# Query and key split into float16 parts once, in the feature-major stage, and copied per head in the attention; GpSimd makes two of eight high parts of the probabilities

## The chip, the core and the metric

The kernel runs on one core of one Trainium2 chip. The core has five engines that work beside each other, each through its own list of instructions in a fixed order: TensorE (PE, matrix products, results go to PSUM), VectorE (DVE), ScalarE (ACT, functions and copies), GpSimd (POOL, elementwise work in SBUF) and SyncE (SP, which issues the transfers here). Where an instruction needs the result of another engine, it waits for a semaphore, and what stands behind it in its list waits too. The metric is the device time of one execution in microseconds.

## What is computed

One encoder layer for 1024 tokens of width 1024 in float32: a modulated RMS norm, one input projection, two groups of heads, an output projection, and a gated residual.

```python
xn = rmsnorm(h, norm_g) * (1 + scale) + shift          # scale, shift, gate from c
proj = xn @ w_in
u_pool, g_pool, q_lat, kv_lat, k_rope_raw, g_attn = split(proj)
y_pool = multiscale_pool(u_pool) * silu(g_pool)        # 4 groups of 128 channels, windows 2, 4, 8, 16
q = rmsnorm(q_lat) @ w_uq ; kv = rmsnorm(kv_lat) @ w_ukv     # 8 heads, q and k of 96 = 64 + 32 rotary
q, k = rmsnorm(q), rmsnorm(k) ; rotary on the last 32
o = softmax(q @ k.T * 96**-0.5) @ v                    # dense, all 1024 positions
y = concat(y_pool, o * silu(g_attn)) @ w_out
out = h + gate * y
```

The precision of float32 is kept by splitting operands in a high and a low part and summing three products: high by high, high by low, low by high. In the attention the parts are float16, elsewhere they are a 32-bit format of TensorE.

## The kernel before, in words

Tokens are tiled by 128 (t from 0 to 7) where features lie along a row ("token-major"), and features by 128 where tokens lie along a row ("feature-major"). The program has these stages, one behind the other on TensorE:

1. **Latents.** The normed input is split into `xh` and `xl`, and the 416 latent columns of the projection are made token-major.
2. **Up-projection** (`up_tok`, one call a token tile). From the latents come q (`QT`, 8 token tiles by 8 heads by 96, float32), the 64 plain features of k (`KT`, the same shape) and v. The sums of squares for the per-head norms are gathered, and `up_norm` makes the factors `rqk`.
3. **Feature-major stage.** The other 12 column tiles of the projection. Tiles 2g and 2g+1 are gate and input of pooling group g, tiles 8 to 11 the gates of the attention. `fm_mm` issues 48 matmuls of 128x512 for a tile (L170): 8 slices of the contraction, for each the products (`whi`,`xh`), (`whi`,`xl`), (`wlo`,`xh`), for two halves of the tokens. The weights come in by a transfer, ScalarE rounds the high part (`whi`, L147), VectorE subtracts for the low one (`wlo`, L148). Both have two buffers, so the weights of tile i can be split once TensorE has done tile i-2. GpSimd multiplies the raw weights by `shift` and folds them (L152, L154), and a small matmul turns the result into the tile's bias (`psb`, L160). `rb_mul` (L527) takes a tile out of PSUM. For the pooling input of group g that is the tile `u`; GpSimd adds its shifted copies, one add more in each group (`s`, L609 and L614), VectorE finishes the means (L617, L618, L621), ScalarE and VectorE split the result (`dh` L624, `dl` L625), and `pool_map` multiplies it on TensorE (`pps`, L640) and into the gate (L641). Between these stand the calls of `up_tail(t)`, eight in all: VectorE multiplies q and k of token tile t by their norm factors and turns the rotary part, in place in `QT` and `KT` (seven instructions, L644 to L654).
4. **Attention.** Eight heads of eight jobs each; a job is 128 queries by all keys (jobs 0 to 3 of a head) or 256 keys by 512 queries (jobs 4 to 7). For each head the parts of q and k must first be made, token-major in a pair of tiles (`src00`, `src01` for even heads, `src1h`, `src1l` for odd ones), and turned by transposing transfers (`turn`). `conv_hi` rounds a head's columns of `KT` or `QT` to float16 (L705 on ScalarE, L707 on VectorE), `conv_lo` subtracts to get the low part (L711). For heads 0 and 1 this is done on the way into the attention, for head h+2 in steps 4 to 7 of head h: VectorE rounds k at step 4 and q at step 6, GpSimd subtracts one half of a tile at each of the four steps. Column 0 of a tile holds one extra row, a bound for the scores, which `prep_max` finds (L730, L733) at four steps of the head before.
   For job i: `scores` (six matmuls, L800 or L804, in two buffers of PSUM; in jobs 0 to 3 a maximum by VectorE, L808 and L809), one step later `expo` (ScalarE, L819: the probabilities p, float32), two steps later `p_hi` (ScalarE rounds p to float16, `ph`, L824) and `p_lo` (the rest, L831, on GpSimd; on VectorE for jobs 1 and 7, whose p lies in PSUM), and six steps later `attend` (L849, L850). `out_copy` (L868, L869) and `out_norm` (L875, L879) finish four jobs. In the last head the parts of the output projection's operands are made beside it (`out_split` L935, L937; `y_split` L914, L916, L918).
5. **Output projection**, eight tiles of 128 features, and the residual.

From the up-projection to the start of the attention the order of each engine's list is set by a scheduler when the program is built: it goes by its own estimates of what is ready when. In the latents and from the attention on (`manual_schedule`) the list is as the loops write it. Pools of buffers set the rest: the feature-major tiles and the `pps` take turns in seven banks of PSUM, `u`, `ra` and `rbt` have one buffer each, and p in SBUF has three.

## Time and profile before

| | us |
|---|---|
| median of 3 runs | 500.09 (499.56 to 500.47) |
| the profiled execution, its own time | 500.05 |
| its span, first to last instruction | 498.3 |
| busy: PE, DVE, ACT, POOL | 464.9, 355.9, 253.8, 234.4 |
| feature-major stage | about 115 to 222 |
| attention | about 225 to 410 |
| output projection | to the end |

All times in the profile count from the start of the span, which leaves 1.75 us of the execution's own time outside. Matmuls are pipelined, so a row's duration on TensorE overlaps that of the next; the distance from start to start is what one costs. The same holds, for less than a tenth of a microsecond, on VectorE. What stands in square brackets behind a row is how long the engine sat idle before it, and what ended that.

### The profile page before, as it was taken

To read this page: it belongs to the slowest core of one execution; us is meant where nothing else is said; L and a number is where in the kernel's file an instruction comes from. 1 tells how busy PE (TensorE), PEld (TensorE's weight loads), DVE (VectorE), ACT (ScalarE), POOL (GpSimd) and SP (SyncE) were. 2 spreads that over 40 slices of the span, in tenths; PEclk is the share of its full clock that TensorE was granted. 3 is DMA by queue.
4 is the path that set the end of the run, shared out by engine and by line. 5 is a ranking of instruction groups with operands and counts; after the bars stand their busy time and mean duration, and the time that the engine had idled before them with its cause. 6 is when DMAs were issued, how large, how long until landed. Compare 5 with 4: busy or idle time off the path is not lost.

```text
span 498.3 us, 7657 instructions
## 1 busy us (share of the span) xinstructions
PE 464.9 (93%) x2956; PEld 355.0 (71%) x2956; DVE 355.9 (71%) x565; ACT 253.8 (51%) x338; POOL 234.4 (47%) x190
## 2 busy tenths in 40 slices
PE   5999998999999999999989888898898969999997
PEld 3999876898888888785555555555555658888886
DVE  4888849999999853577677887877867985913221
ACT  3756038993203030226878888888899861001000
POOL 1950040201242949448869796787869780000000
PEclk9999999999999999999999999999999999999999
DMA  8894442000102110144786779779982836753333
GB/s 300 332 307 159 171 142 65 6 1 7 47 1 91 34 58 27 57 86 95 170 148 138 162 145 176 152 151 163 224 175 63 160 113 231 276 182 129 126 128 126
DMA packets 117046, 66.33 MB, mean 133 GB/s; under 512 B 105873, under 2 KB 107793, under 8 KB 117010
## 3 DMA queue, kind: packets, MB, share of 16 engines
q1 hardware_dynamic: 117010, 65.85, 49.9%
q8 instruction: 23, 0.38, 0.3%
q14 instruction: 13, 0.11, 0.1%
HBM read 35.43 MB, written 4.19 MB: 80 GB/s over the span
## 4 chain that ended last, share of the span: by engine, by line
PE 49%; DVE 22%; ACT 10%; POOL 10%; issue 5%; DMA 3%; SPq 0%; ACTq 0%; DVEq 0%; POOLq 0%
PE ops L974 14%; PE fps L170 8%; PE st L800 4%; PE pq L548 3%; ACT ph L824 3%; PE lps L234 3%; DVE bp L808 3%; POOL fraw L152 3%; ACT p L819 3%; DMA wlr<-in_w_lat 2%; PE rs L730 2%; PE av L849 2%; PE st L804 2%; POOL s L614 2%; DVE ph L831 2%
## 5 line engine op out<-in xcount | busy, mean ns | idle before, releaser
L831 POOL TENSOR_TENSOR ph<-p,ph 128x1024 f16<-128x1024 f32 x49 | 105.9, 2168 | 13.1 <-ACT ph L824 10.2
L170 PE MATMUL fps<-xh,whi 128*128 128x512 f32 x192 | 62.0, 404 | 0.5 <-ACT whi L147 0.5
L170 PE MATMUL fps<-xh,wlo 128*128 128x512 f32 x192 | 59.3, 390 | 0.1
L170 PE MATMUL fps<-xl,whi 128*128 128x512 f32 x192 | 59.3, 390 | 0.0
L800 PE MATMUL st<-q,k 97*128 97x512 f16 x192 | 49.5, 379 | 6.7 <-ACT p L819 6.6
L804 PE MATMUL st<-k,q 97*128 97x512 f16 x192 | 48.2, 379 | 8.0 <-ACT p L819 6.4
L824 ACT ACTIVATE ph<-p 128x1024 f16<-128x1024 f32 x49 | 51.7, 1055 | 0.5
L152 POOL TENSOR_TENSOR fraw<-fraw,shift 128x1024 f32<-128x1024 f32 x7 | 22.7, 3237 | 60.8 <-DVE wlo L148 53.8
L808 DVE TENSOR_REDUCE bp<-st 128x1 f32<-128x1024 f32 x32 | 39.0, 1220 | 5.2 <-PE st L804 3.4
L170 PEld LDWEIGHTS fps<-xh,whi 128*128 128x128 f32 x192 | 35.5, 189 | 9.0 <-ACT whi L147 1.0
L170 PEld LDWEIGHTS fps<-xh,wlo 128*128 128x128 f32 x192 | 36.0, 188 | 8.1 <-DVE wlo L148 0.5
L170 PEld LDWEIGHTS fps<-xl,whi 128*128 128x128 f32 x192 | 36.1, 188 | 7.7
L935 ACT ACTIVATE owhi<-oraw 128x1024 fp32r<-128x1024 f32 (+1 forms) x10 | 8.8, 885 | 54.0 <-DMA oraw<-in_w_out 54.0
L819 ACT ACTIVATE p<-st,bp,esc 128x1024 f32<-128x1024 f32 x25 | 30.1, 1204 | 9.4 <-DVE bp L809 9.0
L804 PEld LDWEIGHTS <-q 97*128 97x128 f16 x192 | 16.6, 97 | 25.6 <-issue 10.9
L800 PEld LDWEIGHTS <-k 97*128 97x128 f16 x192 | 16.6, 97 | 21.5 <-issue 8.3
L624 ACT ACTIVATE dh<-s 128x1024 fp32r<-128x1024 f32 x4 | 4.2, 1062 | 51.9 <-DVE s L621 51.9
L819 ACT ACTIVATE p<-st,ebias,esc 128x1024 f32<-128x1024 f32 x24 | 28.9, 1203 | 2.5 <-PE st L800 1.3
L850 PE MATMUL av<-VT,ph 128*128 128x65 f16 x256 | 26.4, 193 | 2.9 <-POOL ph L831 2.9
L849 PE MATMUL av<-VT,pt 128*128 128x129 f16 x256 | 28.0, 221 | 0.8 <-DMA pt<-ph 0.8
L849 PE MATMUL av<-VT,ph 128*128 128x129 f16 x256 | 27.7, 221 | 0.2 <-DVE rb L869 0.2
L850 PEld LDWEIGHTS <-ph 128*128 128x128 f16 x256 | 22.6, 98 | 7.1 <-POOL ph L831 3.1
(297 smaller groups left out, 1142.5 us busy)
## 6 DMA issues: line engine op xcount, KB each, us to landing
fraw<-in_w_fm SPq DMA_DIRECT2D x12, 512.0 KB, 3.7
asc<-in_ada_sc SPq DMA_DIRECT2D x8, 512.0 KB, 6.0
xr<-in_xT SPq DMA_DIRECT2D x8, 512.0 KB, 5.3
ash<-in_ada_sh SPq DMA_DIRECT2D x8, 512.0 KB, 6.8
oraw<-in_w_out SPq DMA_DIRECT2D x8, 512.0 KB, 5.1
xres<-in_xT SPq DMA_DIRECT2D x8, 512.0 KB, 5.0
agt<-in_ada_gt SPq DMA_DIRECT2D x8, 512.0 KB, 5.7
out_dram<-xres SPq DMA_DIRECT2D x7, 512.0 KB, 3.0
```

The costliest lines, as they stand in the source:

```text
L152: G.tensor_tensor(pb, pb, shift.unsqueeze(2).broadcast_to([P, NK, P]), ALU.mult)
L170: T.matmul(ps[n], w[:, k, :], x_[k][:, n * 512:(n + 1) * 512], start=(k == order[0] and j == 0), stop=(k == order[-1] and j == 2))
L234: T.matmul(ps[:, :LAT], l[k][:, ts_], r[k], start=(k == 0 and i == 0), stop=(k == NK - 1 and i == 2))
L800: T.matmul(stt[i][:, n], l[:HW, kt * P:(kt + 1) * P], r[:HW, 0:512], start=(a == 0), stop=(a == 2))
L804: T.matmul(stt[i][:, n], l[:HW, qt * P:(qt + 1) * P], r[:HW, n * 512:(n + 1) * 512], start=(a == 0), stop=(a == 2))
L808: V.tensor_reduce(bps[i], stt[i], AX.XY, ALU.max)
L819: A.activation(pfs[i], st, AF.Exp, bias=bps.pop(i) if hf else ebias, scale=esc)
L824: A.activation(pas[i][:, 0], pfs[i], AF.Copy)
L831: (V if in_psum(i) else G).tensor_tensor(pas[i][:, 1], pfs[i], pas[i][:, 0], ALU.subtract)
L849: T.matmul(o_, hi, VT[:, kt, h, 0:129], start=kt == 0 and qt % 2 == 0, stop=False, skip_group_check=True)
L850: T.matmul(o_[:, 0:65], lo, VT[:, kt, h, 0:65], start=False, stop=kt == NK - 1, skip_group_check=True)
L974: T.matmul(ps[d][n], w_[:, k, :], y_[k][:, n * 512:(n + 1) * 512], start=(k == 0 and j == 0), stop=(k == NK - 1 and j == 2))
```

## The change

`up_tail` no longer works in place. For q and then for k of a token tile it builds the normed and turned values in a new float32 tile (`fq` or `fk`, one buffer that both share). ScalarE then rounds that tile to float16 and VectorE subtracts, and the two float16 parts are written over the float32 row of `QT` or `KT`, which is twice as wide: first the high parts of all heads, then the low ones. In the attention, `conv_hi` and `conv_lo` are replaced by `gather`, a copy of both parts of a head, float16 to float16, 1536 elements a partition: on VectorE for head 0 and, at steps 4 and 6, for head h+2, on ScalarE for head 1. GpSimd's four half-tile subtractions in each of six heads are gone. `p_hi` of jobs 3 and 5 of a head (`HG`), from the second head on, moves from ScalarE to GpSimd.

```diff
+HG = (3, 5)
...
+    def halves(w, t):
+        return (QT, KT)[w][:, t].rearrange("p h d -> p (h d)").bitcast(F16).rearrange(
+            "p (a h d) -> p a h d", a=2, h=H)
+
     def up_tail(t):
-        V.tensor_tensor(QT[:, t], QT[:, t], rqk[:, 0, t, :].unsqueeze(2).broadcast_to([P, H, HD]), ALU.mult)
-        V.tensor_tensor(KT[:, t, :, 0:64], KT[:, t, :, 0:64],
-                        rqk[:, 1, t, :].unsqueeze(2).broadcast_to([P, H, 64]), ALU.mult)
-        V.tensor_tensor(KT[:, t, :, 64:], krr[:, t, :].unsqueeze(1).broadcast_to([P, H, 32]),
-                        rqk[:, 1, t, :].unsqueeze(2).broadcast_to([P, H, 32]), ALU.mult)
...
+        for w in range(2):
+            f_ = dp.tile([P, H, HD], F32, tag="fq", name=f"f{'qk'[w]}{t}")
+            if w == 0:
+                V.tensor_tensor(f_, QT[:, t], rqk[:, 0, t, :].unsqueeze(2).broadcast_to([P, H, HD]), ALU.mult)
...
+                V.tensor_tensor(ra, f_[:, :, 64:], TA[:, t, :].unsqueeze(1).broadcast_to([P, H, 32]), ALU.mult)
+                V.tensor_tensor(rbt, f_[:, :, 64:], TB[:, t, :].unsqueeze(1).broadcast_to([P, H, 32]), ALU.mult)
+                V.tensor_tensor(f_[:, :, 64:80], ra[:, :, 0:16], rbt[:, :, 16:32], ALU.subtract)
+                V.tensor_tensor(f_[:, :, 80:96], ra[:, :, 16:32], rbt[:, :, 0:16], ALU.add)
+            else:
...
+            p_ = halves(w, t)
+            A.activation(p_[:, 0], f_, AF.Copy)
+            V.tensor_tensor(p_[:, 1], f_, p_[:, 0], ALU.subtract)
...
-    def conv_hi(h, w, eng, t0=0, t1=NK):
-        o_, i_ = srcs[h % 2][w][:, 0, t0:t1, 1:HW], (QT, KT)[w][:, t0:t1, h, :]
+    def gather(h, w, eng):
+        i_ = (QT, KT)[w].rearrange("p t h d -> p (t h d)").bitcast(F16).rearrange(
+            "p (t a h d) -> p a t h d", t=NK, a=2, h=H)[:, :, :, h, :]
+        o_ = srcs[h % 2][w][:, :, :, 1:HW]
...
-    def conv_lo(h, w, eng, t0=0, t1=NK):
...
     for w in (1, 0):
-        conv_hi(0, w, V)
-        conv_lo(0, w, V)
+        gather(0, w, V)
         turn(0, w)
...
-        conv_hi(1, w, A)
-        conv_lo(1, w, G)
+        gather(1, w, A)
...
     def p_hi(i):
...
-        A.activation(pas[i][:, 0], pfs[i], AF.Copy)
+        if i % 8 in HG and i > 7:
+            G.tensor_copy(pas[i][:, 0], pfs[i])
+        else:
+            A.activation(pas[i][:, 0], pfs[i], AF.Copy)
...
             if step % 2 == 0:
-                conv_hi(h + 2, 3 - step // 2, V)
-            conv_lo(h + 2, 3 - step // 2, G, step % 2 * 4, step % 2 * 4 + 4)
+                gather(h + 2, 3 - step // 2, V)
```

The scheduler puts the longer tails elsewhere. Line numbers of the changed kernel are used in the rows of the change. TensorE's list is the same in both kernels. On VectorE, late in the feature-major stage, these rows stand before the change between the weights of tile 8 and the means of pooling group 3 (`u3` is that group's input, `wlo9` the low weights of tile 9):

```order
L148 TENSOR_TENSOR wlo8_1669<-fraw8_1666,whi8_1668 128x1024
L527 TENSOR_TENSOR u3_1738<-fps7_0_1672,rb_79 128x512
L527 TENSOR_TENSOR u3_1738<-fps7_1_1673,rb_79 128x512
L641 SCALAR_TENSOR_TENSOR yp2_1226<-pps20_1728,small_64,yp2_1226 128x512
L641 SCALAR_TENSOR_TENSOR yp2_1226<-pps21_1733,small_64,yp2_1226 128x512
L148 TENSOR_TENSOR wlo9_1788<-fraw9_1785,whi9_1787 128x1024
```

And these in the change, up to `u3`:

```order
L149 TENSOR_TENSOR wlo8_1699<-fraw8_1696,whi8_1698 128x1024
L653 TENSOR_TENSOR fq5_1788<-QT_797,rqk_114 128x768
L656 TENSOR_TENSOR ra5_1790<-fq5_1788,TA_111 128x256
L657 TENSOR_TENSOR rbt5_1791<-fq5_1788,TB_112 128x256
L658 TENSOR_TENSOR fq5_1788<-ra5_1790,rbt5_1791 128x8x16
L659 TENSOR_TENSOR fq5_1788<-ra5_1790,rbt5_1791 128x8x16
L667 TENSOR_TENSOR QT_797<-fq5_1788,QT_797 128x768
L661 TENSOR_TENSOR fk5_1798<-KT_798,rqk_114 128x8x64
L663 TENSOR_TENSOR fk5_1798<-krr_113,rqk_114 128x8x32
L667 TENSOR_TENSOR KT_798<-fk5_1798,KT_798 128x768
L653 TENSOR_TENSOR fq6_1803<-QT_797,rqk_114 128x768
L528 TENSOR_TENSOR u3_1768<-fps7_0_1702,rb_79 128x512
```

Before, all eight tails stood ahead of `u3`, all but the last rows of tail 7 ahead of `u2`; now tail 5 and the first row of tail 6 stand between `wlo8` and `u3`, and tails 6 and 7 behind it. Right behind an L663 or L659 the row L667 waits for ScalarE's copy of the tile just written.

On ScalarE the rounding of tile 10's weights stood behind one function of a gate:

```order
L624 ACTIVATE dh3_1754<-s3_3_1749 128x1024
L676 ACTIVATE gT0_1848<-gT0_1848,bias_fm_80 128x1024
L147 ACTIVATE whi10_1854<-fraw10_1852 128x1024
```

In the change two of the new copies stand among these:

```order
L625 ACTIVATE dh3_1784<-s3_3_1779 128x1024
L666 ACTIVATE KT_798<-fk6_1813 128x768
L689 ACTIVATE gT0_1896<-gT0_1896,bias_fm_80 128x1024
L666 ACTIVATE QT_797<-fq7_1818 128x768
L148 ACTIVATE whi10_1902<-fraw10_1900 128x1024
```

`whi10` has moved behind the copy of `fq7`, whose rows on VectorE stand behind those of tail 6 and around the two rows that take tile 8 (`gT0`) out of PSUM.

On GpSimd in the attention, steps 4 to 7 of the second head (`ph112` is the low part of job 2 of head 1, `ph113` of job 3, `ph100` to `ph102` of jobs 4 to 6), before:

```order
L711 TENSOR_TENSOR src1l_2046<-KT_798,src1l_2046 128x4x96
L831 TENSOR_TENSOR ph112_2439<-p112_2407,ph112_2439 128x1024
L711 TENSOR_TENSOR src1l_2046<-KT_798,src1l_2046 128x4x96
L831 TENSOR_TENSOR ph113_2494<-p113_2442,ph113_2494 128x1024
L711 TENSOR_TENSOR src1h_2045<-QT_797,src1h_2045 128x4x96
L831 TENSOR_TENSOR ph100_2514<-p100_2492,ph100_2514 128x1024
L711 TENSOR_TENSOR src1h_2045<-QT_797,src1h_2045 128x4x96
```

and in the change:

```order
L843 TENSOR_TENSOR ph112_2478<-p112_2447,ph112_2478 128x1024
L834 CAST ph113_2532<-p113_2481 128x1024
L843 TENSOR_TENSOR ph113_2532<-p113_2481,ph113_2532 128x1024
L843 TENSOR_TENSOR ph100_2551<-p100_2530,ph100_2551 128x1024
L891 TENSOR_TENSOR op0_2442<-rb_79,rec00_2582 128x4x64
L834 CAST ph101_2587<-p101_2549 128x1024
L843 TENSOR_TENSOR ph101_2587<-p101_2549,ph101_2587 128x1024
```

The low part of job 2 no longer stands behind a subtraction that waits for VectorE's rounding of k, and two new casts stand ahead of the low parts of jobs 3 and 5.

More of the change, by code (lines that the diff above doesn't have):

```diff
@@ L647, in up_tail @@
-        V.tensor_tensor(KT[:, t, :, 64:], krr[:, t, :].unsqueeze(1).broadcast_to([P, H, 32]),
-                        rqk[:, 1, t, :].unsqueeze(2).broadcast_to([P, H, 32]), ALU.mult)
-        ra = dp.tile([P, H, 32], F32, tag="ra", name=f"ra{t}")
-        rbt = dp.tile([P, H, 32], F32, tag="rbt", name=f"rbt{t}")
-        V.tensor_tensor(ra, QT[:, t, :, 64:], TA[:, t, :].unsqueeze(1).broadcast_to([P, H, 32]), ALU.mult)
-        V.tensor_tensor(rbt, QT[:, t, :, 64:], TB[:, t, :].unsqueeze(1).broadcast_to([P, H, 32]), ALU.mult)
@@ L653, in up_tail @@
-        V.tensor_tensor(QT[:, t, :, 64:80], ra[:, :, 0:16], rbt[:, :, 16:32], ALU.subtract)
-        V.tensor_tensor(QT[:, t, :, 80:96], ra[:, :, 16:32], rbt[:, :, 0:16], ALU.add)
+        for w in range(2):
+            f_ = dp.tile([P, H, HD], F32, tag="fq", name=f"f{'qk'[w]}{t}")
+            if w == 0:
+                V.tensor_tensor(f_, QT[:, t], rqk[:, 0, t, :].unsqueeze(2).broadcast_to([P, H, HD]), ALU.mult)
+                ra = dp.tile([P, H, 32], F32, tag="ra", name=f"ra{t}")
+                rbt = dp.tile([P, H, 32], F32, tag="rbt", name=f"rbt{t}")
+                V.tensor_tensor(ra, f_[:, :, 64:], TA[:, t, :].unsqueeze(1).broadcast_to([P, H, 32]), ALU.mult)
[3 more added lines that the diff above has]
+            else:
+                V.tensor_tensor(f_[:, :, 0:64], KT[:, t, :, 0:64],
+                                rqk[:, 1, t, :].unsqueeze(2).broadcast_to([P, H, 64]), ALU.mult)
+                V.tensor_tensor(f_[:, :, 64:], krr[:, t, :].unsqueeze(1).broadcast_to([P, H, 32]),
+                                rqk[:, 1, t, :].unsqueeze(2).broadcast_to([P, H, 32]), ALU.mult)
+            p_ = halves(w, t)
+            A.activation(p_[:, 0], f_, AF.Copy)
+            V.tensor_tensor(p_[:, 1], f_, p_[:, 0], ALU.subtract)
@@ L707, in conv_hi @@
             eng.tensor_copy(o_, i_)
-    def conv_lo(h, w, eng, t0=0, t1=NK):
-        s_ = srcs[h % 2][w]
-        eng.tensor_tensor(s_[:, 1, t0:t1, 1:HW], (QT, KT)[w][:, t0:t1, h, :], s_[:, 0, t0:t1, 1:HW], ALU.subtract)
     def turn(h, w):
```

## The prediction

> **What bounds the kernel now.** I read the busy times by stretch first, then the chain of waits in order of time, then each engine's rows where the chain runs. The feature-major stage from the first row of the first tail (125.56 us) to the low weights of tile 10 (211.43); columns: stretch, length, busy PE, PEld, DVE, ACT, POOL, clock, DMA:
>
> ```profile
> 125.56:211.43 85.87, 85.32 (x378) 69.74 (x377) 65.35 (x111) 15.97 (x15) 47.57 (x31) 1.00 0.14 45
> ```
>
> TensorE looks like the bound. The chain that ended last (start, length, what) says otherwise:
>
> ```profile
> 159.40 10.00 POOL fraw L152
> ...
> 209.13 1.05 ACT whi L147
> 210.20 1.24 DVE wlo L148
> ```
>
> It runs through GpSimd's folds and sums and VectorE to `whi10` and `wlo10`, and tile 10 waits for them. The rows of the engines around it:
>
> ```profile
> 210.22 0.73 PE L170 MATMUL fps<-xh,whi 128*128 128x512 f32 x2 [0.54 <-ACT whi L147]
> 179.05 0.16 DVE L617 TENSOR_TENSOR s<-s,small 128x4 f32<-128x4 f32 x1 [6.21 <-POOL s L614]
> 201.17 1.24 DVE L617 TENSOR_TENSOR s<-s,small 128x8 f32<-128x8 f32 x1 [10.00 <-POOL s L614]
> 134.16 2.39 DVE L645 TENSOR_TENSOR KT<-KT,rqk 128x512 f32<-128x512 f32 x1
> 133.50 2.49 POOL L152 TENSOR_TENSOR fraw<-fraw,shift 128x1024 f32<-128x1024 f32 x1 [3.44 <-DVE wlo L148]
> 185.54 1.90 POOL L152 TENSOR_TENSOR fraw<-fraw,shift 128x1024 f32<-128x1024 f32 x1 [4.71 <-DVE wlo L148]
> 213.54 2.85 POOL L154 TENSOR_TENSOR fraw<-fraw 128x512 f32<-128x512 f32 x3
> ```
>
> TensorE reaches tile 10 only 0.54 us ahead of its weights: a VectorE that comes later has no cover there. VectorE is idle for 85.87 - 65.35 = 20.5 us of the stretch, but most of it is two waits for GpSimd's sums (6.21 and 10.00). And the two engines hold each other up: L152 takes 1.90 us alone and 10.00 beside VectorE's tails (159.40); L645 takes 2.39 beside an L152, and 0.68 in the next fence. A whole fold alone is 1.90 + 2.85 = 4.75.
>
> **The tails.** An undisturbed token tile; the distance from start to start is what a row costs:
>
> ```profile
> 139.38 0.94 DVE L644 TENSOR_TENSOR QT<-QT,rqk 128x768 f32<-128x768 f32 x1
> 140.25 0.28 DVE L653 TENSOR_TENSOR QT<-ra,rbt 128x128 f32<-128x128 f32 x1
> ...
> 140.66 0.68 DVE L645 TENSOR_TENSOR KT<-KT,rqk 128x512 f32<-128x512 f32 x1
> 141.26 0.41 DVE L647 TENSOR_TENSOR KT<-krr,rqk 128x256 f32<-128x256 f32 x1
> 141.59 0.41 DVE L651 TENSOR_TENSOR ra<-QT,TA 128x256 f32<-128x256 f32 x1
> ...
> 142.26 1.28 DVE L527 TENSOR_TENSOR u<-fps,rb 128x512 f32<-128x512 f32 x2
> ```
>
> A tail is 142.26 - 139.38 = 2.88 us of VectorE. The forms that the change adds (a subtraction to float16, a copy to float16) stand in the making of heads 0 and 1; with them come the handover from VectorE to ScalarE and back, and the other rows that the sum needs:
>
> ```profile
> 217.60 0.95 DVE L711 TENSOR_TENSOR src<-QT,src 128x768 f16<-128x768 f32 x1
> 218.47 1.21 DVE L148 TENSOR_TENSOR wlo<-fraw,whi 128x1024 fp32r<-128x1024 f32 x1
> 224.81 0.83 ACT L705 ACTIVATE src1h<-QT 128x768 f16<-128x768 f32 x1
> 128.58 1.22 DVE L621 SCALAR_TENSOR_TENSOR s<-s,u 128x1024 f32<-128x1024 f32 x1
> 129.91 1.06 ACT L624 ACTIVATE dh<-s 128x1024 fp32r<-128x1024 f32 x1 [2.83 <-DVE s L621]
> 131.01 1.23 DVE L625 TENSOR_TENSOR dl<-s,dh 128x1024 fp32r<-128x1024 f32 x1
> 148.87 0.21 DVE L633 CAST pwh<-pwr 128x128 fp32r<-128x128 f32 x1
> 185.38 1.28 DVE L527 TENSOR_TENSOR u<-fps,rb 128x512 f32<-128x512 f32 x2
> 186.57 1.41 DVE L641 SCALAR_TENSOR_TENSOR yp<-pps,small,yp 128x512 f32<-128x512 f32 x2
> 208.07 1.15 ACT L676 ACTIVATE gT<-gT,bias_fm 128x1024 f32<-128x1024 f32 x1 [2.62 <-DVE gT L527]
> ```
>
> A subtraction costs 218.47 - 217.60 = 0.87 us, two a tail: 2.88 + 1.74 = 4.62. ScalarE has room (15.97 us busy of 85.87), but its copy stands between VectorE's last row on `fq` or `fk` and the subtraction: 0.11 us to ScalarE (L621 ends at 129.80, L624 starts at 129.91), 0.83 for the copy, 0.04 back (130.97 to 131.01). The row ahead is busy 0.41 where its follower could start after 0.33, so a wait that nothing fills is 0.08 + 0.98 = 1.06 us. `fq` and `fk` share one buffer and VectorE's list is fixed, so only what the scheduler put between can fill it. Nothing stands between for k of tiles 0, 4 and 5 and for q of tiles 3 and 5: five bare waits ahead of `u3`.
>
> I add up VectorE's time in three sections.
>
> *First tail to the end of `u3`*: 125.56 to 186.66 before, 61.1 us. Eight tails stood in it (8 x 2.88 = 23.0); now six and one row (6 x 4.62 + 0.87 = 28.6): +5.6. Five bare waits: +5.3. The wait for group 2's sums (6.21) shrinks, because VectorE comes to it later: behind `u2` GpSimd needs three sums of 1.95 (next fence), 5.85, and up to 2.0 more while VectorE's subtraction and `wlo7` run; VectorE fills 3.4 of it (L641 1.4, subtraction 0.87, `wlo7` 1.14). That leaves 2.5 to 4.5; I take 4.4, because L152's 10.00 shows GpSimd giving way: -1.8. The blocking elsewhere I keep as it was. Together +9.1: `u3` ends near 195.8.
>
> *`u3` to group 3's sums*: 186.66 to 201.17 before, 14.5 us, with the fold of tile 8 and a part of tile 9's in the way.
>
> ```profile
> 190.98 1.97 POOL L609 TENSOR_TENSOR s<-u 128x1038 f32<-128x1038 f32 x1
> 193.02 3.90 POOL L614 TENSOR_TENSOR s<-s 128x1036 f32<-128x1036 f32 x2
> ```
>
> Now the fold of tile 8 is over by then and that of tile 9 stands behind the sums. Four sums are 1.97 + 3 x 1.95 = 7.8 us, and up to 2.5 more beside `ra` and `rbt` (0.67), `wlo9` (1.14), two rotary rows (0.41) and the pool weights (some 0.35). I take 9.8, towards the upper end as above: -4.7.
>
> *The sums to the end of `wlo10`*: 201.17 to 211.43 before, 10.3 us. VectorE now does edges and mean (1.28), subtracts q of tile 6 (0.87), does `fk6` and `dl3` (0.60 + 1.14 + 0.33), waits (1.06), subtracts (0.87), starts `fq7` (0.87), takes tile 8 out of PSUM (1.2) with `ra` and `rbt` between (0.67): 8.9. Then ScalarE's gate (0.11 + 1.06), the copy of `fq7` (0.8), `whi10` (1.05), and `wlo10` (1.24): 13.2. Of blocking by a fold the old section held 1.1 (L617 1.24 at 201.17, 0.16 at 179.05), and tile 9's fold still runs beside it, so I keep 1.1: 14.3, +4.0.
>
> Sum: 9.1 - 4.7 + 4.0 = **+8.4 us**, all of it TensorE's, which waits at tile 10. Lower bound: GpSimd's rows all slip into the new waits (group 2's wait falls by 4.4 more, the second section to 7.8, no blocking in the third): 8.4 - 4.4 - 2.0 - 1.1 = +0.9. Upper bound: the fold of tile 8 slips behind `u3` and that of tile 9 blocks fully: 8.4 + 4.75 + 3.65 = +16.8. I stay in the middle; it is nearest to the blocking that the trace has.
>
> Between tile 10 and the attention, the last tail, its waits and two copies in place of two casts and two subtractions cost VectorE some 1.5 us more. The cover is the 2.7 us for which the turned q of head 0 lay ready (221.95 to 224.67):
>
> ```profile
> 219.72 2.23 SPq L722 DMA_TRANSPOSE q<-src  x1
> ...
> 224.67 0.61 PE L730 MATMUL rs<-k,q 97*128 97x512 f16 x2
> ```
>
> If that cover were gone it would be +1.5; I take 0. ScalarE's two wider copies for head 1 replace GpSimd's subtractions behind the same casts: 0.
>
> **The attention.** ScalarE loses two casts a head, GpSimd trades four half subtractions (0.86 each) for two casts. The question is whether TensorE waits for these. Rows from two neighbouring heads, and one from the last:
>
> ```profile
> 281.52 0.56 DVE L707 CAST src<-KT 128x768 f16<-128x768 f32 x1
> 265.48 2.25 DVE L707 CAST src1h<-QT 128x768 f16<-128x768 f32 x1
> 265.17 2.14 POOL L831 TENSOR_TENSOR ph<-p,ph 128x1024 f16<-128x1024 f32 x1
> 280.02 1.06 ACT L824 ACTIVATE ph<-p 128x1024 f16<-128x1024 f32 x1
> 282.15 0.86 POOL L711 TENSOR_TENSOR src<-KT,src 128x384 f16<-128x384 f32 x1 [3.15 <-DVE src L707]
> 268.91 0.59 PE L730 MATMUL rs<-k,q 97*128 97x512 f16 x2 [0.53 <-DVE src L733]
> 275.02 1.46 PE L804 MATMUL st<-k,q 97*128 97x512 f16 x6 [1.19 <-ACT p L819]
> 280.04 0.81 PE L800 MATMUL st<-q,k 97*128 97x512 f16 x3 [0.88 <-ACT p L819]
> 407.67 0.20 PE L850 MATMUL av<-VT,ph 128*128 128x65 f16 x1 [2.95 <-POOL ph L831]
> ```
>
> TensorE's two long waits of a head (1.19, 0.88) are for the exponentials of jobs 0 and 2, which stand behind the high parts of jobs 7 and 1 on ScalarE. The casts that leave it are those of jobs 3 and 5: gain 0.
>
> The copy of k is where VectorE may lose. Before, GpSimd was idle there (3.15), waiting for the rounding, which took 0.56. Now the low part of job 2 can start when ScalarE's row of 280.02 ends (281.08), ahead of VectorE at 281.52, and runs 2.1 us. VectorE would stand until 283.2, 1.7 us, as its rounding of q stood behind the L831 of 265.17 (2.25 in place of 0.56). The maxima behind it (L733) come late by that, but TensorE already waits 0.53 for them later in the head, and the wait of q's copy gets shorter as that of k's grows, since the low part of job 3 is then further on. I take +0.3 a head for six heads, +1.8; bounds -0.5 a head (the 0.53 gone) and +1.7 a head.
>
> The copy has twice the elements of the cast; from L633 (128 elements, 0.21) to L707 (768, 0.56) an element costs 0.55 ns, so 1536 take 0.56 + 0.42 = 0.98, between 0.56 if that is bytes and not elements, and 0.95 + 768 x 1.02 ns = 1.73 if it runs like the two-input rows (0.95 for 768, 1.21 for 1024). I take 0.98, by the row that is also a copy in SBUF; the 0.4 more is in the +0.3. GpSimd's cast of 1024 lies between 0.86 (a row of 384) and 2.14; half of the two-input row, 1.1, is nearest for one input. Two of them fit in the four subtractions' 3.4. In the last head, where no subtractions were, GpSimd ends TensorE's wait of 2.95; the casts take 2.2 us more there, but in place of waits for ScalarE: -1 to +2, I take 0.
>
> Attention: **+1.8**, bounds -3 and +10 to +12.
>
> [...]
>
> **Sum.** The profiled execution took 500.05 us, the median is 500.09, so nothing is to be corrected: 500.05 + 8.4 + 1.8 = 510.3, say **510**.
>
> **Rivals.**
> - *The slack takes it.* The new work is 16 x 0.87 = 13.9 us and VectorE idles 20.5. For it speaks the idle time, against it that this is waiting for sums which start behind `u3`, and `u3` moves back. Then the lower bounds hold: 500.05 + 0.9 - 3 = 498.
> - *Half of it.* GpSimd's folds slip into the new waits, the sums start as they did after `u3`: +4, attention 0: 504.
> - *The copy of k decides in every head.* 500.05 + 8.4 + 6 x 1.7 = 518.7. It decides once the low part of job 2 starts ahead of the copy by more than VectorE's gaps in these steps (0.53 and the like) can take.
>
> **Chances.** Forecast (506 to 515) 0.58, half 0.17, copy of k 0.12, slack 0.13. The range that leaves out 2 in 10 is 502 to 516. About 1 us, 0.2%, is what a measurement of this kernel can tell from no change: of the slack's 0.13 I give 0.09 to faster and 0.04 to the same; all the rest, 0.87, is slower.
>
> **What would show it.** Right: `u3` (L528) ends near 196 and `wlo10` (L149) near 220, TensorE stands some 8 us more ahead of tiles 9 and 10, VectorE waits about 1 us for L666 in five to eight places, and the attention's length stays within 2 us, with L722 for k at over 2 us. Wrong: `wlo10` ends before 214; or TensorE's waits for the exponentials of jobs 0 and 2 shrink though only casts of jobs 3 and 5 left ScalarE; or L722 for k grows and the heads grow with it.

## The result, and the profile after

The changed kernel takes 516.45 us (median of 6 runs, 515.73 to 518.25), the kernel before, measured beside it, 500.28 (499.56 to 503.08, 6 runs): a ratio of 1.032, 95% interval 1.029 to 1.035. The forecast was 510, with a range of 502 to 516. The sign is right, the size is about 6 us short, and the time lies just above the range. The profiled execution of the change has a span of 514.0 us, 15.7 more than before.

The three sections of the feature-major stage that the prediction summed, in the changed kernel (stretch, length, busy PE, PEld, DVE, ACT, POOL, clock, DMA): first tail to the end of `u3`, to the first row on group 3's sums, to the end of `wlo10`:

```profile
124.81:199.59 74.78, 72.77 (x321) 59.36 (x321) 65.89 (x97) 22.26 (x24) 29.41 (x23) 1.00 0.13 40
199.59:212.41 12.82, 6.01 (x20) 4.50 (x19) 12.79 (x11) 0.84 (x1) 12.35 (x6) 0.73 0.07 27
212.41:226.76 14.35, 9.27 (x40) 6.74 (x38) 11.73 (x20) 4.73 (x5) 2.27 (x2) 1.00 0.10 37
sum 101.95, PE 88.06 PEld 70.60 DVE 90.41 ACT 27.84 POOL 44.03; mean PE 29.35 PEld 23.53 DVE 30.14 ACT 9.28 POOL 14.68
```

TensorE was busy for 85.32 of 85.87 us of this stage before; now it is for 88.06 of 101.95. It stands still for 13.9 us, at these places (rows of TensorE with what it waited for, the last one at the start of the attention):

```profile
174.62 0.74 PE L171 MATMUL fps<-xh,wlo 128*128 128x512 f32 x2 [0.93 <-DVE wlo L149]
...
199.05 0.50 PE L171 MATMUL fps<-xh,whi 128*128 128x512 f32 x1 [0.96 <-DVE u L528]
206.82 1.22 PE L171 MATMUL fps<-xh,wlo 128*128 128x512 f32 x2 [6.80 <-DVE wlo L149]
220.86 0.35 PE L161 MATMUL psb<-ones,fraw 128*128 128x1 f32 x2 [2.27 <-DVE bias_fm L162]
225.55 0.74 PE L171 MATMUL fps<-xh,whi 128*128 128x512 f32 x2 [2.82 <-ACT whi L148]
242.50 0.61 PE L741 MATMUL rs<-k,q 97*128 97x512 f16 x2 [0.85 <-DMA q<-src]
```

What VectorE did around these waits, rows in order of time:

```profile
193.51 0.96 DVE L667 TENSOR_TENSOR QT<-fq,QT 128x768 f16<-128x768 f32 x1 [0.91 <-ACT QT L666]
...
196.44 0.96 DVE L667 TENSOR_TENSOR KT<-fk,KT 128x768 f16<-128x768 f32 x1 [0.91 <-ACT KT L666]
197.44 0.96 DVE L653 TENSOR_TENSOR fq<-QT,rqk 128x768 f32<-128x768 f32 x1
198.31 1.28 DVE L528 TENSOR_TENSOR u<-fps,rb 128x512 f32<-128x512 f32 x2
...
201.79 2.13 DVE L657 TENSOR_TENSOR rbt<-fq,TB 128x256 f32<-128x256 f32 x1
203.84 2.92 DVE L149 TENSOR_TENSOR wlo<-fraw,whi 128x1024 fp32r<-128x1024 f32 x1
206.69 2.46 DVE L658 TENSOR_TENSOR fq<-ra,rbt 128x128 f32<-128x128 f32 x1
209.07 1.98 DVE L659 TENSOR_TENSOR fq<-ra,rbt 128x128 f32<-128x128 f32 x1
...
212.41 0.15 DVE L618 TENSOR_TENSOR s<-s,small 128x8 f32<-128x8 f32 x1
```

`u3` (L528 at 198.31) comes 12.9 us later than before (185.38). Behind it stands no wait for GpSimd's sums any more, where 10.00 us stood. Instead four rows, one behind the other, take 1.98 to 2.92 us each, about as long as one of GpSimd's sums (1.92, 1.97, 1.96 and 3.24): L658 takes 2.46 us, against 0.28 in a quiet place, and `wlo9` 2.92 against 1.22. GpSimd ran its four sums in the same time:

```profile
199.68 1.92 POOL L610 TENSOR_TENSOR s<-u 128x1038 f32<-128x1038 f32 x1 [6.76 <-DVE u L528]
201.67 7.33 POOL L615 TENSOR_TENSOR s<-s 128x1036 f32<-128x1036 f32 x3
```

From here on a row's **hold-up** is its duration less the shortest that a row of its form has in any run of this study, added up over rows; differences of less than 0.05 us, which rows show without GpSimd's work too, are left out, and a sum holds to some 0.2 us. A row's own price, under "rows", is that shortest duration less 0.09 us, for the overlap with the next; "gaps" is what remains. VectorE's time in the first section, worked out in this way (us):

| kernel | length | rows | held up | waits for sums | waits for ScalarE | gaps |
|---|---|---|---|---|---|---|
| before | 61.1 | 45.3 | 7.3 | 6.2 | 0.8 | 1.5 |
| change | 74.8 | 50.8 | 12.1 | 3.6 | 4.9 | 3.4 |

In the second section VectorE is held up for 8.9 us (1.6 before). Over the whole way to the copy of q for head 0 it is 23.5 us against 11.1.

### The profile page after: what moved, and what is told of

It is laid out like the page before. It is cut to its first block, busy times and chain, and to the rows that moved or that the text cites. A ratio compares the mean times of both kernels' runs of the same rounds, so it can differ in the third digit from the quotient of the medians.

```text
span 514.0 us, 7647 instructions
## 1 busy us (share of the span) xinstructions
PE 469.2 (91%) x2956; PEld 356.4 (69%) x2956; DVE 384.2 (75%) x579; ACT 255.1 (50%) x340; POOL 227.1 (44%) x178
## 4 chain that ended last, share of the span: by engine, by line
PE 53%; DVE 24%; ACT 9%; POOL 6%; DMA 4%; issue 3%; SPq 0%; ACTq 0%; DVEq 0%; POOLq 0%
PE ops L986 14%; PE fps L171 8%; PE st L809 6%; PE st L813 5%; PE av L861 3%; PE pq L549 3%; ACT p L828 3%; PE rs L741 2%; POOL ph L843 2%; DMA wlr<-in_w_lat 2%; PE lps L235 2%; DVE fq L653 2%; PE pk L559 2%; ACT ph L836 2%; DVE wlo L149 2%
## 5 line engine op out<-in xcount | busy, mean ns | idle before, releaser
L843 POOL TENSOR_TENSOR ph<-p,ph 128x1024 f16<-128x1024 f32 x49 | 107.2, 2194 | 39.4 <-ACT ph L836 35.2
L171 PE MATMUL fps<-xh,wlo 128*128 128x512 f32 x192 | 61.2, 401 | 7.9 <-DVE wlo L149 7.7
L171 PE MATMUL fps<-xh,whi 128*128 128x512 f32 x192 | 63.4, 411 | 3.8 <-ACT whi L148 2.8
L153 POOL TENSOR_TENSOR fraw<-fraw,shift 128x1024 f32<-128x1024 f32 x7 | 16.3, 2330 | 71.9 <-DVE wlo L149 59.8
L836 ACT ACTIVATE ph<-p 128x1024 f16<-128x1024 f32 x35 | 36.9, 1054 | 0.5
L809 PEld LDWEIGHTS <-k 97*128 97x128 f16 x192 | 16.5, 97 | 21.2 <-issue 7.3
L744 DVE TENSOR_REDUCE src<-rs 128x1 f16<-128x1024 f32 x16 | 19.6, 1224 | 10.1 <-PE rs L741 9.3
```

The source lines that it names most:

```text
L153: G.tensor_tensor(pb, pb, shift.unsqueeze(2).broadcast_to([P, NK, P]), ALU.mult)
L171: T.matmul(ps[n], w[:, k, :], x_[k][:, n * 512:(n + 1) * 512], start=(k == order[0] and j == 0), stop=(k == order[-1] and j == 2))
L744: V.tensor_reduce(s_[:, 0, qt, 0:1], ps, AX.XY, ALU.max, negate=True)
L809: T.matmul(stt[i][:, n], l[:HW, kt * P:(kt + 1) * P], r[:HW, 0:512], start=(a == 0), stop=(a == 2))
L836: A.activation(pas[i][:, 0], pfs[i], AF.Copy)
L843: (V if in_psum(i) else G).tensor_tensor(pas[i][:, 1], pfs[i], pas[i][:, 0], ALU.subtract)
```

## The experiments

Times are medians, ratios go against the kernel before, each with its 95% interval. Diffs are against the changed kernel where nothing else is said. The first theory was that VectorE is now the bound, by its subtractions, its waits for ScalarE and more blocking by GpSimd than I had allowed for.

**Two buffers for `fq` and `fk`.**

```diff
-            f_ = dp.tile([P, H, HD], F32, tag="fq", name=f"f{'qk'[w]}{t}")
+            f_ = dp.tile([P, H, HD], F32, tag=f"f{w}", name=f"f{'qk'[w]}{t}")
```

> The changed kernel with a buffer of its own for fq and one for fk, so that q of a tile need not wait for k's subtraction and the other way round. Theory (VectorE is the bound of the feature-major stage, by its subtractions, its bare waits for ScalarE and the blocking by GpSimd): most of the waits of 0.91 us for L666 fill with other rows, eight to ten of them, so wlo10 ends 4 to 8 us earlier than 226.8 and the time is 508 to 513. Rival A (the waits for ScalarE are nearly all of the loss): 500 to 506. Rival B (the order of VectorE's list decides, u3 stands one tail further back in it here): 516 or more.

513.35 us, 1.026 (1.021 to 1.031). VectorE's waits for ScalarE in the first section fall from 4.9 to 1.7 us, but `u3` ends no earlier (its section is 76.3 us): held up 9.7, waits for sums 6.8. Waits for ScalarE are not nearly all of the loss, so rival A falls. The theory's 508 to 513 was just missed, and `wlo10` ends at 224.2, only 2.6 us earlier where it had 4 to 8.

**The high part on VectorE.**

```diff
-            A.activation(p_[:, 0], f_, AF.Copy)
+            V.tensor_copy(p_[:, 0], f_)
```

> The changed kernel with the high part of q and k copied by VectorE instead of ScalarE: no handover, but 16 copies of 0.56 us (9 us) more on VectorE. Theory (VectorE bound): 16 copies of 0.5 us come on and eight to ten waits of 0.91 go, so about the same, 514 to 518. Rival A (the waits for ScalarE are nearly all): 505 to 510. Rival C (what GpSimd takes from VectorE is the larger part, and a copy waits for GpSimd as other rows do): over 518.

520.14 us, 1.040 (1.037 to 1.043). There is no wait for ScalarE left in the first section (4.9 us in the changed kernel), but with the copies (0.55 us each where nothing holds them up) it is 79.4 us long, 17.7 of them hold-ups. The theory's "about the same" was missed; rival C's number came in.

**No low part, first attempt.**

```diff
-            V.tensor_tensor(p_[:, 1], f_, p_[:, 0], ALU.subtract)
+            A.activation(p_[:, 1], f_, AF.Copy, scale=0.0)
```

> The changed kernel without the subtractions of the low part in the feature-major stage: ScalarE writes zeros there (so the low parts of q and k are left out of the result). VectorE loses 16 x 0.87 = 13.9 us and its waits for the high part. Theory (VectorE bound): the whole delay of the stage goes, 498 to 502. Rival C (GpSimd's blocking of the small rotary rows is the larger part, and these rows stay): half of it goes, 506 to 510.

ScalarE writes zeros in place of the low parts. 510.44 us, 1.020 (1.016 to 1.025). This is near rival C's 506 to 510, but the run doesn't tell: with one buffer, VectorE now waits for two copies of ScalarE in place of one:

```profile
165.26 0.69 DVE L661 TENSOR_TENSOR fk<-KT,rqk 128x512 f32<-128x512 f32 x1 [1.65 <-ACT QT L667]
167.93 0.96 DVE L653 TENSOR_TENSOR fq<-QT,rqk 128x768 f32<-128x768 f32 x1 [1.65 <-ACT KT L667]
```

In the first section 12 us of such waits took the place of the subtractions. So it was run again with two buffers:

> The changed kernel without the subtractions of the low part (ScalarE writes zeros, the low parts of q and k are left out of the result) and with a buffer each for fq and fk, so that the second copy on ScalarE does not hold VectorE up as it did with one buffer (waits of 1.65 us). Theory (subtractions, waits for ScalarE and what is queued behind them make the delay): 498 to 503. Rival C (blocking of the rotary rows by GpSimd is the larger part, whatever VectorE has to do besides): 506 or more.

499.60 us, 0.998 (0.995 to 1.002). Against the 513.35 with two buffers and the subtractions (two runs, 512.31 and 514.39) these cost 13.75 us, 16 x 0.86: every one at about its full price, although VectorE had idle time. In the profiled executions the first scores come 12.75 us earlier (227.04 against 239.79).

**The order of VectorE's list.** Two edits: the weights ahead, and the tails of tiles 5 to 7 queued behind `u3` (`u_last[3]` is the last row that takes `u3` out of PSUM).

```diff
-            fm_w[i + 1] = fm_weights(i + 1)
+            with tc.high_priority():
+                fm_w[i + 1] = fm_weights(i + 1)
```

> The changed kernel with the weight rows (copy to whi, subtraction to wlo) given precedence in the scheduler, so that wlo9 stands on VectorE ahead of the rotary rows of tile 6 that wait for GpSimd's sums. Theory (VectorE's whole list up to wlo10 bounds): TensorE's wait of 6.80 us for wlo9 goes, and the wait at tile 10 grows by as much; the time stays within 2 us, 514 to 518. Rival B (the order of the list decides): 6.8 us less, 509 to 511.

```diff
-        if gi:
+        if gi == 3:
+            with tc.issue_after(u_last[gi]):
+                up_tail(2 * gi - 1)
+                up_tail(2 * gi)
+        elif gi:
             up_tail(2 * gi - 1)
             up_tail(2 * gi)
-    up_tail(7)
+    with tc.issue_after(u_last[3]):
+        up_tail(7)
```

> The changed kernel with the tails of token tiles 5, 6 and 7 queued on VectorE behind u3, as far as u3 allows; nothing else is changed. In the changed kernel TensorE had finished tile 7 near 185 us, but u3 came only at 198.3, since the fixed list has it behind tail 5. Theory (VectorE's whole work up to the copies of head 0 bounds): u3 ends near 189, wlo10 by 214, TensorE's waits at tiles 9 and 10 nearly go, but the tails are then unfinished: the copies of head 0 end near 232 and the first scores come at 236 to 240 instead of 242.5, so 510 to 514. Rival B (the order of the list decides): the first scores near 230, 501 to 505. Rival D (the order is without effect): 516.

519.57 us, 1.039 (1.032 to 1.045), and 519.18 us, 1.036 (1.033 to 1.039). In the first, TensorE's wait for `wlo9` shrinks from 6.80 to 0.77 us and `wlo10` ends at 225.6 instead of 226.8, but TensorE then waits 9.29 us for VectorE at the small matmul of a bias (220.44); nothing is won, and the time is above the 514 to 518 that I expected. In the second `u3` comes at 187.85. The delay only moves, to VectorE's wait for the sums and to TensorE's first scores:

```profile
202.70 1.84 DVE L621 TENSOR_TENSOR s<-s,small 128x8 f32<-128x8 f32 x1 [6.27 <-POOL s L618]
...
244.06 1.04 PE L749 MATMUL rs<-k,q 97*128 97x512 f16 x2 [9.76 <-DMA q<-src]
```

Neither order helps, which fits the theory that VectorE's whole list up to the copies of head 0 decides. My own 510 to 514 for the second was too low, since the fold of tile 8 came to stand ahead of the sums on GpSimd.

**Without GpSimd's work.** The sums, and the folds from tile 4 on, left out in both kernels:

```diff
-            fm_fold(pb)
+            if i < 4:
+                fm_fold(pb)
...
-        s_ = gp.tile([P, S + 16], F32, tag="gT0", name=f"s{gi}_0")
-        G.tensor_tensor(s_[:, 1:S + 15], u[:, 0:S + 14], u[:, 1:S + 15], ALU.add)
-        lo_, m = 1, 1
-        for lev in range(gi):
+        s_ = u
+        for lev in ():
```

> The changed kernel without GpSimd's running sums (the unsummed tile takes their place) and without its folds from tile 4 on, so the pooled branch and the biases are left out of the result. Against the kernel before with the same left out. Theory (some 7 us of the delay is VectorE's small rows waiting for GpSimd, the rest subtractions and waits for ScalarE): this kernel loses both the waits for the sums and the blocking and comes to 500 to 506, 2 to 8 us above its counterpart. Rival A (subtractions and waits for ScalarE alone): 508 or more, over 10 us above its counterpart.

> The kernel before with the same left out (GpSimd's running sums, and its folds from tile 4 on). TensorE was busy for 85.3 of 85.9 us of the feature-major stage, so nothing is to be had there: 497 to 500 by every theory.

497.96 us, 0.994 (0.992 to 0.996), and 499.20 us, 0.996 (0.995 to 0.998). This is the central pair: without these rows of GpSimd the change costs nothing in the stage, with all 16 subtractions, all rounding on ScalarE and the single buffer as they are. (It is even some 1.2 us faster, and that comes behind the first scores: 271.65 us from there to the end against 274.08.) Nor is it the order of the list: as in the changed kernel, tails 0 to 5 and the first row of tail 6 stand ahead of `u3`. VectorE still has waits of 0.91 us, but they lie beside TensorE's tiles; it takes `u3` out of PSUM at 185.17:

```profile
183.31 0.96 DVE L666 TENSOR_TENSOR KT<-fk,KT 128x768 f16<-128x768 f32 x1 [0.91 <-ACT KT L665]
...
185.17 0.68 DVE L529 TENSOR_TENSOR u<-fps,rb 128x512 f32<-128x512 f32 x1
```

TensorE's waits on the way to the attention come to 0.5 us, as in the kernel before the change, and the first scores come at 224.51 (224.67 before the change). So "subtractions and waits for ScalarE" is no cause by itself, and my own theory, which left 2 to 8 us between the two kernels, fell short as well. Half of GpSimd's work was left out next, by one of the two edits each:

> The changed kernel without GpSimd's folds from tile 4 on (the biases are left out of the result); the running sums stay. Theory now (VectorE's rows with two inputs from SBUF wait for GpSimd's instructions, 23.5 us in the changed kernel against 11.1 before, from the first tail to the copy of q of head 0; subtractions and waits for ScalarE alone fit into VectorE's idle time): folds and sums are each about half of GpSimd's work, so the excess falls to about half, 10 to 14 us, and the time to 500 to 506. Rival E (the sums alone do it, since they stand in the chain): 510 or more.

> The changed kernel without GpSimd's running sums (the unsummed tile takes their place, so the pooled branch is left out of the result); the folds stay. Theory: excess of VectorE 8 to 12 us, no waits for the sums, 498 to 503. Rival E (the sums alone do it): 498, with hardly any excess left beside the folds.

502.27 us, 1.003 (1.001 to 1.005), and 501.54 us, 1.001 (0.999 to 1.003). Leaving out either half is enough to come within 2 us of the kernel before, so it isn't the sums alone (rival E). Hold-ups to the copy of q are 9.5 and 14.6 us, where I had expected 10 to 14 and 8 to 12.

**GpSimd's work in shorter pieces.** The same work, each sum and the multiplication of each fold in four parts, the first addition of a fold in two:

```diff
-        G.tensor_tensor(pb, pb, shift.unsqueeze(2).broadcast_to([P, NK, P]), ALU.mult)
+        for a in range(0, NK, NK // 4):
+            b = a + NK // 4
+            G.tensor_tensor(pb[:, a:b], pb[:, a:b], shift[:, a:b].unsqueeze(2).broadcast_to([P, b - a, P]), ALU.mult)
...
+        def g_add(o, a, b, l, h):
+            cs = [l + (h - l) * i // 4 for i in range(4 + 1)]
+            for x, y in zip(cs, cs[1:]):
+                G.tensor_tensor(o[:, x:y], s_in[:, x - a:y - a], s_in[:, x + b:y + b], ALU.add)
...
-            G.tensor_tensor(n_[:, l2:h2], s_[:, l2 - m:h2 - m], s_[:, l2 + m:h2 + m], ALU.add)
+            s_in = s_
+            g_add(n_, m, m, l2, h2)
```

> The changed kernel with every running sum and every fold of GpSimd cut into pieces (sums and the multiplication of a fold into four, its first addition into two), the same work in shorter instructions; nothing is left out. Theory F (a row of VectorE waits until the running GpSimd instruction is over, one instruction each in turn): a blocked row loses some 0.5 us instead of up to 2, VectorE's excess falls from 23.5 to 6 to 12 us and the time to 501 to 508. Rival G (the two share one rate, and only the sum of their work counts): excess 20 or more, 514 to 518.

> The same cut of GpSimd's work and a buffer each for fq and fk. Theory F with the waits for ScalarE filled: 498 to 504, at or below the kernel before. Rival G: 511 to 515, as with two buffers alone.

513.86 us, 1.027 (1.025 to 1.029), and with two buffers 516.25 us, 1.031 (1.029 to 1.033). In the first, the single hold-up shrinks as theory F had it: beside the fold of tile 8 a rotary row takes 0.8 us where it took 2.00 (L656 at 188.22 in the change):

```profile
190.50 0.83 DVE L668 TENSOR_TENSOR rbt<-fq,TB 128x256 f32<-128x256 f32 x1
...
191.87 0.82 DVE L670 TENSOR_TENSOR fq<-ra,rbt 128x128 f32<-128x128 f32 x1
```

Hold-ups up to the copy of q fall from 23.5 to 13.5 us, just above F's 12, but the time by only 2.6, since the sums come later: VectorE's waits for them in the first section rise from 3.6 to 7.7 us. Hold-ups plus waits for sums are 15.2 us there with the cut and 15.7 without. Rival G came nearest on the time (514 to 518) though not on the hold-ups (20 or more); F was right about the row. With two buffers both missed: the time is above G's 511 to 515, and hold-ups plus waits for sums are 18.6 us in the first section, 10.8 of them waits.

**16 rows more in the kernel before**, which has no rounding on ScalarE in its tails: with two inputs from SBUF, or with one, at the same places of the list.

```diff
         V.tensor_tensor(QT[:, t, :, 80:96], ra[:, :, 16:32], rbt[:, :, 0:16], ALU.add)
+        for w in range(2):
+            scr = dp.tile([P, H, HD], F32, tag="scr", name=f"scr{w}{t}")
+            V.tensor_tensor(scr, QT[:, t], KT[:, t], ALU.subtract)
```

and with one input, in place of the last line:

```diff
+            V.tensor_reduce(scr[:, 0, 0:1], QT[:, t], AX.XY, ALU.max)
```

> The kernel before with 16 rows more on VectorE in the tails (one behind each half of a tail): a subtraction of 768 elements with both inputs in SBUF, 0.87 us each, 13.9 us in all, into a scratch tile that nobody reads; no ScalarE is asked. Theory H (VectorE's rows with two SBUF inputs and GpSimd's rows share one resource: 84.2 us of 90.4 were taken in the kernel before, 100.6 of 110.7 in the changed one): 98 us are wanted where some 87 are there, so 510 to 515. Rival A (the waits for ScalarE in the changed kernel): 500 to 503, since there are none here.

> The same with a row of one SBUF input in place of the subtraction: a maximum over the same 768 elements, about 0.87 us each, at the same places of VectorE's list. Theory H: VectorE has idle time and GpSimd isn't held up, 500 to 504. Rival I (it is VectorE's time alone that is short, whatever its rows read): as with two inputs, 510 to 515.

513.43 us, 1.025 (1.021 to 1.030), and 513.31 us, 1.025 (1.021 to 1.030). They pay 12.7 and 12.6 us for 16 x 0.87 = 13.9. Rival A falls for good: no handover to ScalarE is in these. Theory H as I put it falls too, since the row with one input should have been nearly free, and rival I's number (VectorE's time alone is short) came in. But VectorE's time alone it can't be, since without GpSimd's work the change's rows cost nothing. In the rows the two kinds differ all the same. At the same place, beside GpSimd's sums of group 2, with two inputs:

```profile
173.86 1.57 DVE L657 TENSOR_TENSOR scr<-QT,KT 128x768 f32<-128x768 f32 x1
175.35 2.93 DVE L148 TENSOR_TENSOR wlo<-fraw,whi 128x1024 fp32r<-128x1024 f32 x1
180.08 0.17 DVE L617 TENSOR_TENSOR s<-s,small 128x4 f32<-128x4 f32 x1 [1.80 <-POOL s L614]
```

and with one:

```profile
173.25 0.94 DVE L657 TENSOR_REDUCE scr<-QT 128x1 f32<-128x768 f32 x1
174.11 1.21 DVE L148 TENSOR_TENSOR wlo<-fraw,whi 128x1024 fp32r<-128x1024 f32 x1
179.12 0.16 DVE L617 TENSOR_TENSOR s<-s,small 128x4 f32<-128x4 f32 x1 [3.80 <-POOL s L614]
```

The row with one input isn't held up there (0.94 against 1.57), and the `wlo` behind it gets by (1.21 against 2.93). But VectorE then waits 3.80 instead of 1.80 us for the sums. In these rows, what isn't lost in hold-ups is lost in the wait, and the first section is as long in both: 76.2 and 76.3 us.

**Relief, computing the same.** The multiplication of the folds from tile 4 on ScalarE, as eight rows with a scale for each partition, and two buffers; then q's scaling too; then the tails of tiles 6 and 7 queued behind `u3` besides.

```diff
-        G.tensor_tensor(pb, pb, shift.unsqueeze(2).broadcast_to([P, NK, P]), ALU.mult)
+        if on_a:
+            for k in range(NK):
+                A.activation(pb[:, k], pb[:, k], AF.Copy, scale=shift[:, k:k + 1])
+        else:
+            G.tensor_tensor(pb, pb, shift.unsqueeze(2).broadcast_to([P, NK, P]), ALU.mult)
...
-            fm_fold(pb)
+            fm_fold(pb, i > 3)
...
-                V.tensor_tensor(f_, QT[:, t], rqk[:, 0, t, :].unsqueeze(2).broadcast_to([P, H, HD]), ALU.mult)
+                for h in range(H):
+                    A.activation(f_[:, h], QT[:, t, h], AF.Copy, scale=rqk[:, 0, t, h:h + 1])
```

> The changed kernel with a buffer each for fq and fk (513.35 with that alone) and the multiplication of the folds of tiles 4 to 10 moved from GpSimd to ScalarE, as eight short rows with a scale for each partition; the result is the same. GpSimd loses some five rows of 1.95 us on the way to the attention. Theory H: 99.3 - 9.7 = 89.6 us, near what was there before, so 502 to 507. Rival G of the run with shorter pieces (nothing but the whole of GpSimd's chain counts): 510 to 514.

> The same, and the scaling of q as well on ScalarE (eight rows of 96 elements a tail in place of VectorE's 0.87 us), so VectorE loses another 7 us with two SBUF inputs. Theory H: some 83 us are wanted, less than TensorE's 87, so 497 to 502, about the kernel before or just below it. Rival A (handovers between VectorE and ScalarE): 505 or more, since each tail now starts with one.

> The kernel with the fold's multiplication and the scaling of q on ScalarE and two buffers (503.3), and besides with the tails of token tiles 6 and 7 queued on VectorE behind u3. There VectorE now arrives at u3 about 9 us after TensorE has finished tile 7 (fps7 near 185, u3 at 194.4) and stands in no queue of its own work worth 9 us behind it. Theory (VectorE's own rows, what GpSimd holds up, and the waits, have to fit between TensorE's tiles; they do once u3 doesn't stand behind tails that have time): TensorE's waits ahead of tiles 9 and 10 (3.2 and 1.8 us) go, first scores near 225, 497 to 500, at or below the kernel before. Rival D (the deferred tails come back as a wait ahead of the first scores, as they did without the other measures): 502 to 506.

509.79 us, 1.019 (1.016 to 1.022); 503.32 us, 1.005 (1.003 to 1.007); 503.47 us, 1.005 (1.004 to 1.007). Theory H gave less time in both of the first two (502 to 507, 497 to 502), and I expected 497 to 500 of the third; all three missed. Work taken off GpSimd is worth 3.6 us, less than its 9.7; work taken off VectorE (8 x 0.87 = 7.0) is worth 6.5, nearly its full price. The third brings nothing: `u3` comes at 186.30 as meant, but the fold of tile 8, which waits for ScalarE, now stands ahead of the sums, and VectorE waits for these again, so rival D's number came in by another way (GpSimd's row, then VectorE's):

```profile
190.20 4.09 POOL L159 TENSOR_TENSOR fraw<-fraw 128x512 f32<-128x512 f32 x3 [10.57 <-ACT fraw L155]
```

```profile
202.65 0.17 DVE L625 TENSOR_TENSOR s<-s,small 128x8 f32<-128x8 f32 x1 [9.50 <-POOL s L622]
```

No version that computes the whole beats the kernel before.

**GpSimd's high parts undone.**

```diff
-        if i % 8 in HG and i > 7:
+        if False:
```

> The changed kernel with the high parts of p of jobs 3 and 5 back on ScalarE; the split of q and k and the copies per head stay. Theory (TensorE waits for the exponentials of jobs 0 and 2, which the casts of jobs 3 and 5 don't touch): 515 to 518, as the changed kernel; the gain of 2 us in the attention comes from the copies alone. Rival (taking two casts off ScalarE is where the attention's 2 us come from): 518 to 520; or GpSimd's casts cost: 511 to 514.

519.92 us, 1.038 (1.036 to 1.040), some 3 us above the changed kernel (1.029 to 1.035, measured at another time). I expected no difference; the number of the first rival came in. From the first scores to the end it is 273.8 us here, 271.5 in the changed kernel and 273.6 before; every run of this study with the casts on GpSimd takes 270.6 to 272.9 there, those without 273.4 to 274.7. Which wait it comes from I can't show. The three largest of TensorE's waits in the attention (line, waited for, us in total, times, longest), here:

```profile
PE st L809 <- ACT p L828: 6.3, 8, 0.9
PE st L813 <- ACT p L828: 6.3, 7, 1.2
PE av L862 <- POOL ph L843: 2.9, 1, 2.9
```

and in the changed kernel:

```profile
PE st L813 <- ACT p L828: 6.5, 7, 1.2
PE st L809 <- ACT p L828: 6.3, 8, 0.9
PE av L861 <- DVE rb L881: 2.1, 1, 2.1
```

The two waits for exponentials don't shrink, as I had said; the 2.3 us are spread over small differences. The rows show a candidate other than ScalarE. With the casts on GpSimd the copy of q takes 0.56 us, without them it is held up in five heads (1.69 to 2.07 us), as in this row:

```profile
305.46 1.69 DVE L722 COPY src<-QT 128x1536 f16<-128x1536 f16 x1
```

VectorE's maxima stand behind these copies, and TensorE's waits for those (`src`, `src1h`, L744) come to 3.4 us here and 2.4 in the changed kernel: 1.0 of the 2.3 us. That the copies cause it is not shown.

## Why the prediction was right in sign and too small

- **Rows of the tails**: +5.6 forecast for the first section, +5.5 measured (50.8 - 45.3). The subtraction takes 0.96 as read.
- **Waits for ScalarE**: five of 1.06 ahead of `u3`, +5.3 forecast; +4.1 measured (4.9 - 0.8). The five are there, a bare wait being 0.91.
- **The step that failed is GpSimd's share**, "The blocking elsewhere I keep as it was", together with "-1.8" for the shorter wait for sums. I took these for two things. The wait shrank (6.2 to 3.6), but hold-ups rose by 4.8: +2.2 in place of -1.8, 4.0 us too little. The runs show that the two trade against each other: hold-ups plus waits for sums are 13.5 us in the first section before, 15.7 in the change, 16.5 with two buffers, 15.2 with GpSimd cut, 16.1 and 16.2 with 16 rows more in the kernel before, and at most 0.2 without GpSimd. The sum is no constant: it is 17.7 with the high part on VectorE and 18.6 with GpSimd cut and two buffers. Gaps between rows that need the row just ahead, +1.9, I had not counted.
- **Second section**: 9.8 forecast with "up to 2.5 more" for blocking, 12.8 measured. The sums were done near 209, but VectorE's small rows, each held up behind a row of GpSimd, ended at 212.4: 8.9 us of hold-ups. The same mistake, 3.0 us.
- **Third section**: 14.3 forecast, 14.35 measured, through the rows that the forecast names.
- **Behind tile 10**: "I take 0"; +2.5 measured from the end of `wlo10` to the first scores (15.74 against 13.24). It is VectorE's: from `wlo10` to the transfer that turns k of head 0 it takes 8.89 us against 6.33, where I had 1.5 more; a row of the last tail alone is held up for 1.7 (0.41 in a quiet place). And the cover of 2.7 us was misread. The row of 219.72 shows the issue of the transfer, not its landing. That of k, issued at 217.76, landed 4.4 us later; in the change q is issued at 237.66, and TensorE waits for it until 242.50, 2.7 us behind the end of that row (2.6 to 2.8 in the five other runs in which TensorE waits for q):

```profile
227.28 2.12 DVE L663 TENSOR_TENSOR fk<-krr,rqk 128x256 f32<-128x256 f32 x1
...
235.65 1.89 SPq L733 DMA_TRANSPOSE k<-src  x1
237.66 2.16 SPq L733 DMA_TRANSPOSE q<-src  x1
```

  By the same distance q landed near 224.6 in the kernel before, an estimate, just when TensorE needed it (224.67). By this there was no cover.
- **Attention**: +1.8 forecast, -2.1 measured. The copies without the casts on GpSimd: +0.2 (273.8 against 273.6), although the copy of k is held up as forecast (2.2 to 2.4 us in each head). GpSimd's high parts: -2.3, where I had 0; with them the copy of q is no longer held up, and a free copy takes 0.56, not 0.98. In the changed kernel:

```profile
299.12 2.25 DVE L722 COPY src<-KT 128x1536 f16<-128x1536 f16 x1
304.32 0.56 DVE L722 COPY src<-QT 128x1536 f16<-128x1536 f16 x1
```

The sum: +16.1 in the stage (101.95 - 85.87), which starts 0.75 us earlier, +2.5, -2.1: 15.7, the difference of the spans. That the forecast is only some 6 us short is partly luck: up to the first scores it is 9.4 us short (8.4 against 17.8), and 3.9 too high in the attention.

Beneath the terms lies one reading that was wrong in kind: VectorE's 20.5 us of idle time in the stage. I let the later rows use 6.5 us of it (1.8 and 4.7). Hardly any was free: most of it (6.2 and 10.0 us) was VectorE waiting for sums beside which, as the second section shows, its own rows get through at a fraction of their speed (L658 takes 2.46 us where it has 0.28 in a quiet place). Before, VectorE came to `u3` (185.38) just when TensorE passed on to tile 8 (185.87). Beyond that point a microsecond of VectorE's rows came out as 0.9 to 1 of time in three comparisons, with ScalarE between (13.75 of 13.9) or without (12.7 of 13.9), and where rows were taken away (6.5 of 7.0). Without GpSimd's work the same rows cost nothing. That load on VectorE and GpSimd together does it is shown by the runs that take either away. That no order of the lists could have held more of it is only argued, from four orders.

## To carry to other kernels

Where two engines hold each other up, as VectorE and GpSimd did here, the idle time of one that waits for the other isn't room: add its own rows, what the neighbour holds up and the waits for the neighbour, and compare that sum with the bound's pace. To price such a pair, leave the neighbour's work out in both kernels: if the change then costs nothing, neither its rows nor its handovers are the cause alone. Before one buffer's reader is moved to another engine, ask who frees the buffer afterwards.
